# Queueing the filling work of the scan behind the step's pieces on VectorE, ScalarE and GpSimd as well as on TensorE

## The chip, the core and the metric

The program runs on one core of one Trainium2 chip, in one launch. The metric is device microseconds of one execution. Five engines work side by side, each through its own queue of instructions in a fixed order: TensorE (PE in the profile; PEld is its weight load), VectorE (DVE), ScalarE (ACT), GpSimd (POOL), and SyncE (SP), which here only issues DMAs. An instruction starts when those ahead of it on its engine have started and what it waits for on other engines is done.

## The reference

Two layers of a hybrid encoder over 512 tokens of width 1024. Each layer runs three mixers on one projection of the normalised input, multiplies their concatenated output with `w_out`, and then runs a mixture of 16 experts and a small gate. The part that matters here:

```
y_a = gmlp_spatial_gating(...)            # channels 0..255 of the mixers' output
y_b = dilated_attention(...)              # channels 256..639, 6 heads
y_c = gated_deltanet(...)                 # channels 640..1023, 6 heads, forward and backward scan
x = x + concat([y_a, y_b, y_c]) @ w_out[i]
x = x + expert_choice_ffn(rmsnorm(x, g_ffn[i]), ...)
x = x + rmsnorm(p[i] @ w_ple) * sigmoid(rmsnorm(x) @ w_ple_gate)

def step(state, inp):                     # the scan: each step needs the state of the one before
    v_new = u_n - w_n @ state
    o_n = (q_n * exp(g_n)) @ state + qk_n @ v_new
    state = state * exp(g_last) + (k_n * exp(g_last - g_n)).T @ v_new
```

## The kernel before

Each layer's mixer ends in a scan of 16 steps (chunks of 32 tokens, both directions at once). A step is a chain over four engines, and has too little work to fill any of them, so other work is traced between its pieces. `gdn_scan` is the lead. A step n is three pieces: (1) TensorE multiplies the state with keys and queries (`pK`), VectorE scales it (`tm`) and subtracts it from the values (`rr`); (2) TensorE makes `pV`, ScalarE copies it to `vn`; (3) GpSimd scales the state (`St`, line 961), TensorE makes `pS` and `pO`, VectorE adds into `St` and makes `tmp` or `o_sum`, and from step 8 on GpSimd adds `tmp` into `o_sum` (line 988).

The fill is a chain of three generators: `attn_v` (the attention's values), `core` (the attention: scores `sc`, softmax `P`, transposes `ptp`/`PT`, output `po`, split `yTb`), and `w_out_first`, which multiplies the part of the output that the scan does not make (channels 0..639) with `w_out`. `w_out_first` takes its weights in three pieces of 384, 384 and 256 columns (below: pieces 1, 2 and 3; 128x1920, 128x1920 and 128x1280 elements in SBUF). Pieces 4 and 5 (128x1536 each) are for the scan's own channels, in `w_out_last`. At the start of each piece `wnext` splits the raw weights `w` into a high part `whi` (ScalarE, line 338) and the rest `wlo` = w - whi (GpSimd, line 340), and asks for the next raw piece by DMA. A product with a split operand is three matmuls, by `whi` (line 348), by `wlo` (349), and by `whi` again (350), into the PSUM tile `op`; VectorE adds `op` to `x` (line 1039).

`interleave` pulls three pieces of the fill, and then, after each piece of the lead, as much fill as it owes by a table of weights. What it pulls is traced at once. A scheduler then orders each engine's queue by its own model of time; it may move an instruction ahead of others that were traced before it. `in_order` puts a bound on that for TensorE alone: each piece is traced under `issue_after(last)`, where `last` is the TensorE instruction that the piece before ended with, so on TensorE the pieces stand in the order in which they were pulled. On VectorE, ScalarE and GpSimd nothing holds the order, other than data and buffers.

After the scan, `gdn_out` squares `o_sum` (ScalarE, `sqo`, line 1005), sums it (VectorE, `so`, line 1006), takes a reciprocal root by small VectorE steps (lines 183 to 190, result `ro`), scales and gates `o_sum` (1014, 1015), and transposes it (`ycp`, `yTc`). `w_out_last` then multiplies with pieces 4 and 5, and router and experts follow. All weights share a pool of 12 SBUF slots, which are reused as they come free; ScalarE's split of piece 4 and of piece 5 writes into such a slot.

Of the kernel before, what the change touches and what calls it, by code (L numbers as in the profile page):

```python
# [117 lines left out]
class K:  # L118
# [315 lines left out]

    def in_order(self):

        last = None

        def piece(gen):
            nonlocal last  # L440
            with ExitStack() as st:
                if last is not None:
                    st.enter_context(self.tc.issue_after(last))
                r = next(gen, None)
            ins = self.nc.cur_bb.bb.instructions
            k = len(ins) - 1
            while ins[k] is not last and ins[k].engine != self.nc.tensor.engine:
                k -= 1
            last = ins[k]
            return r  # L450

        return piece

    def interleave(self, lead, fill):


        piece, owed = self.in_order(), 0.0
        for _ in range(INIT):
            piece(fill)
        while True:  # L460
            r = piece(lead)
            if r is None:
                return
            owed += r
            while owed > OWED:
                r = piece(fill)
                if r is None:
                    break
                owed -= r
# [1034 lines left out]
```

## Time and profile before

| what | value |
|---|---|
| three timed runs, median (lowest to highest) | 1958.14 us (1953.76 to 1958.29) |
| the profiled execution, device time | 1962.08 us |
| its span, first to last instruction | 1960.3 us |
| PE busy | 1809.5 us, 92% |
| DVE busy | 931.7 us, 48% |
| ACT busy | 523.9 us, 27% |
| POOL busy | 457.4 us, 23% |
| the chain that ended last, by engine | PE 69%, DVE 20%, ACT 3%, POOL 2% |

The scan with its fill stands at about 228 to 382 us of the span in the first layer and 1196 to 1346 us in the second; the experts take most of the rest. In the rows below, times are microseconds from the start of the span. In a timeline each row is one instruction or a few equal ones in sequence: start, duration from the first's start to the last's end, engine, line, operation, tiles and shapes; in square brackets stands how long the engine was idle before it and what ended that. A window's row gives each engine's busy time in the stretch, and PEclk is the granted TensorE clock as a share of 2.4 GHz: 1.00 is 2.4 GHz, 0.50 is 1.2 GHz, and a value between is a mean over both.

### The profile page before, as it was taken

The page shows a single profiled execution, that of the slowest core. Times are in us where ns is not written, and L with a number is a line of the kernel's source. Part 1 is how long each engine was busy: PE and PEld are TensorE (multiplying, and loading weights), DVE is VectorE, ACT ScalarE, POOL GpSimd, SP SyncE. Part 2 cuts the span into 40 slices and gives each one's busy share as a digit, 9 for nine tenths or more (in the row PEclk, how much of TensorE's full clock was granted, in tenths as well). Part 3 has the DMA queues.
Part 4 walks back from the last instruction along what each step waited for, and adds up shares of the span by engine and source line. Part 5 has one row for each costly group of instructions (what it writes and reads, how often), then busy time and mean ns, then how long its engine had stood idle before and what let it go on. Part 6 is the DMA issues. An engine that isn't in the chain of part 4 may idle for free.

```text
span 1960.3 us, 30038 instructions
## 1 busy us (share of the span) xinstructions
PE 1809.5 (92%) x12216; PEld 1140.4 (58%) x12216; DVE 931.7 (48%) x2088; ACT 523.9 (27%) x1213; POOL 457.4 (23%) x402
## 2 busy tenths in 40 slices
PE   6898698979999999999989978899799999999999
PEld 5777665864344444434988767568544344443358
DVE  5879767671112121132778796776511212114126
ACT  4334444331010101102443344552311011011023
POOL 3544313320000003021645452233100000031025
PEclk9998788989999999999998977999799999999999
DMA  5212020187799999899342020202987999998991
GB/s 169 86 33 60 17 85 15 56 329 302 321 423 421 409 421 407 345 412 379 111 134 76 24 74 2 97 2 102 411 321 318 422 421 397 422 394 345 380 328 66
DMA packets 122394, 467.47 MB, mean 238 GB/s; under 512 B 11664, under 2 KB 68496, under 8 KB 75920
## 3 DMA queue, kind: packets, MB, share of 16 engines
q1 hardware_dynamic: 115168, 458.46, 59.5%
q10 hardware_dynamic: 7088, 7.09, 1.2%
q8 instruction: 96, 1.57, 0.3%
q14 instruction: 42, 0.34, 0.1%
HBM read 461.32 MB, written 4.19 MB: 237 GB/s over the span
## 4 chain that ended last, share of the span: by engine, by line
PE 69%; DVE 20%; ACT 3%; issue 3%; POOL 2%; DMA 2%; ACTq 0%; SPq 0%; DVEq 0%; POOLq 0%
PE pGt L1276 14%; PE pUp L1276 11%; PE pY L1276 10%; DVE acc L778 3%; PE xep L1206 2%; PE ysc L1295 2%; DVE rr L944 2%; PE xep L1207 2%; PE pY L1391 2%; PE pV L951 1%; PE op L348 1%; PE ysc L1296 1%; PE pgp L348 1%; PE pgp L350 1%; PE plep L1172 1%
## 5 line engine op out<-in xcount | busy, mean ns | idle before, releaser
L1276 PE MATMUL pGt<-w,xe 128*64 128x512 f32 x592 | 194.8, 607 | 0.0
L340 POOL TENSOR_TENSOR wlo<-w,whi 128x512 fp32r<-128x512 f32 (+5 forms) x66 | 162.1, 2473 | 102.9 <-ACT whi L338 71.9
L1276 PE MATMUL pUp<-w,xe 128*64 128x512 f32 x688 | 178.4, 593 | 0.0
L1343 POOL TENSOR_TENSOR x<-x,hh 128x1024 f32<-128x1024 f32 x8 | 18.8, 2356 | 620.0 <-DMA wx<-in_w_e_up_dram 310.4
L1276 PE MATMUL pY<-w,hidT 128*64 128x512 f32 x608 | 162.5, 596 | 0.2 <-ACT hidT L1350 0.2
L1360 DVE SCALAR_TENSOR_TENSOR yl<-pY,gsl,yh 128x512 fp32r<-128x512 f32 x28 | 21.0, 751 | 203.1 <-ACT yh L1359 201.5
L1301 DVE TENSOR_TENSOR x<-ysc,x 128x512 f32<-128x512 f32 x96 | 62.9, 686 | 110.5 <-PE ysc L1296 110.5
L1276 PEld LDWEIGHTS pUp<-w,xe 128*64 128x64 f32 x688 | 62.9, 137 | 89.5 <-issue 86.3
L1276 PEld LDWEIGHTS pGt<-w,xe 128*64 128x64 f32 x592 | 56.1, 137 | 99.2 <-issue 92.7
L1276 PE MATMUL pGt<-wx,xe 128*64 128x512 f32 x384 | 113.0, 599 | 0.3
L1334 DVE SCALAR_TENSOR_TENSOR hid<-sg,gsl,pUp 128x512 f32<-128x512 f32 x32 | 23.9, 748 | 169.8 <-PE pUp L1276 168.0
L1276 PEld LDWEIGHTS pY<-w,hidT 128*64 128x64 f32 x608 | 55.6, 136 | 76.2 <-issue 73.3
L1276 PE MATMUL pUp<-wx,xe 128*64 128x512 f32 x320 | 99.8, 595 | 0.0
L1276 PE MATMUL pY<-wx,hidT 128*64 128x512 f32 x288 | 86.2, 595 | 0.0
L1327 DVE SCALAR_TENSOR_TENSOR sg<-sg,pGt 128x512 f32<-128x512 f32 x32 | 21.7, 686 | 131.3 <-ACT sg L1326 131.3
L338 ACT ACTIVATE whi<-w 128x512 fp32r<-128x512 f32 (+5 forms) x66 | 68.2, 1058 | 38.5 <-PE op L349 15.8
L1326 ACT ACTIVATE sg<-pGt,gsl 128x512 f32<-128x512 f32 x32 | 21.8, 687 | 196.5 <-PE pGt L1276 194.6
L1350 ACT ACTIVATE hidT<-htp 128x512 f32<-128x512 f32 x32 | 19.0, 597 | 200.4 <-PE htp L1349 200.4
L1206 PE MATMUL xep<-OH,hh 128*128 128x256 f32 x256 | 70.1, 307 | 2.4 <-DVE OH L1194 2.4
L778 DVE SCALAR_TENSOR_TENSOR acc<-raw,pp,acc 128x512 f32<-128x512 f32 x72 | 64.3, 894 | 15.5 <-ACT acc L776 13.0
L348 PE MATMUL pgp<-whi,gTh 128*128 128x256 f32 x256 | 70.9, 281 | 0.0
L350 PE MATMUL pgp<-whi,gTl 128*128 128x256 f32 x256 | 69.8, 282 | 0.3 <-DVE gTl L279 0.3
(404 smaller groups left out, 4277.3 us busy)
## 6 DMA issues: line engine op xcount, KB each, us to landing
w<-in_w_e_up_dram SPq DMA_DIRECT2D x86, 1024.0 KB, 15.4
w<-in_w_e_down_dram SPq DMA_DIRECT2D x76, 1024.0 KB, 12.7
w<-in_w_e_gate_dram SPq DMA_DIRECT2D x74, 1024.0 KB, 15.6
wx<-in_w_e_gate_dram SPq DMA_DIRECT2D x48, 1024.0 KB, 9.9
wx<-in_w_e_up_dram SPq DMA_DIRECT2D x40, 1024.0 KB, 16.7
wx<-in_w_e_down_dram SPq DMA_DIRECT2D x36, 1024.0 KB, 12.0
wd<-in_w_e_down_dram SPq DMA_DIRECT2D x32, 512.0 KB, 8.3
w<-in_w_in_dram SPq DMA_DIRECT2D x14, 1024.0 KB, 5.2
```

The lines of the kernel that those rows point to most:

```text
L338: self.nc.scalar.activation(rr_(hi[:, ks, :]), wk, AF.Copy)
L340: e.tensor_tensor(rr_(lo[:, ks, :]), wk, hi[:, ks, :], op=ALU.subtract)
L348: pe.matmul(p, lh, rh, start=first, stop=False)
L350: pe.matmul(p, ll, rh, start=False, stop=last)
L778: v.scalar_tensor_tensor(acc, raw[:, kk:kk + S], conv[:, b, kk:kk + 1], acc, op0=ALU.mult, op1=ALU.add)
L944: v.tensor_tensor(rr[kl[dr], :], vtok[kl[dr], tl, :], fl(tm[kl[dr]]), op=ALU.subtract)
L1206: pe.matmul(p, rr_(hh[:, t, ks]), OHf[:, t, :], start=(t == 0), stop=False)
L1207: pe.matmul(p, rr_(hl[:, t, ks]), OHf[:, t, :], start=False, stop=(t == NT - 1))
L1276: pe.matmul(pt[nh][64 * ei:64 * ei + 64, :], lhs[:, kk, 64 * ei:64 * ei + 64], wt[ei][k][:, nh * 512:nh * 512 + 512], start=(kk == 0), sto ...
L1295: pe.matmul(p, rr_(OT[:, t, :]), rr_(yh[:, ns]), start=True, stop=False)
L1301: v.tensor_tensor(xv, p, xv, op=ALU.add)
L1391: pe.matmul(pY[64 * ei:64 * ei + 64, :], hidT[:, 4 * half + k, 64 * ei:64 * ei + 64], wt[ei][:, k, :], start=(half + k == 0), stop=(half * ...
```

## The change

`in_order`'s `piece` gets a flag that says whether the piece is the lead's. After a piece of the lead it notes the last instruction that the piece traced on VectorE, on ScalarE and on GpSimd. Each later piece of the fill is traced under `issue_after` for these three too, so its instructions on an engine queue behind the last piece of the lead that was pulled before it. The lead's own pieces get no such bound against the fill. On TensorE the rule is as before.

```diff
-        last = None
-
-        def piece(gen):
+        last, ahead = None, {}
+
+        def piece(gen, leads=False):
             nonlocal last
+            ins = self.nc.cur_bb.bb.instructions
+            k0 = len(ins)
             with ExitStack() as st:
                 if last is not None:
                     st.enter_context(self.tc.issue_after(last))
+                if not leads:
+                    for i in ahead.values():
+                        st.enter_context(self.tc.issue_after(i))
                 r = next(gen, None)
...
+            for i in ins[k0:]:
+                if i.engine == self.nc.tensor.engine:
+                    last = i
+                elif leads and i.engine in (self.nc.vector.engine, self.nc.scalar.engine, self.nc.gpsimd.engine):
+                    ahead[i.engine] = i
             return r
...
-            r = piece(lead)
+            r = piece(lead, True)
```

Behind `in_order` all line numbers are 8 higher in the changed kernel. What the bound does to the queues is best seen where `w_out_first` starts. On GpSimd, before, the first rows of the scan hold the splits of pieces 1 and 2 (`wlo` 128x1920), among the state's scalings of steps 1 to 9:

```order
L961 TENSOR_TENSOR St<-St,ex 128x384 x5
L340 TENSOR_TENSOR wlo<-w,whi 128x1920
L961 TENSOR_TENSOR St<-St,ex 128x384 x2
L340 TENSOR_TENSOR wlo<-w,whi 128x1920
L961 TENSOR_TENSOR St<-St,ex 128x384 x2
L988 TENSOR_TENSOR o_sum<-tmp,o_sum 32x384 x2
```

and the scan's last rows there, with the splits of pieces 3, 4 and 5, are

```order
L961 TENSOR_TENSOR St<-St,ex 128x384
L988 TENSOR_TENSOR o_sum<-tmp,o_sum 32x384 x2
L340 TENSOR_TENSOR wlo<-w,whi 128x1280
L961 TENSOR_TENSOR St<-St,ex 128x384
L988 TENSOR_TENSOR o_sum<-tmp,o_sum 32x384 x4
L340 TENSOR_TENSOR wlo<-w,whi 128x1536
L988 TENSOR_TENSOR o_sum<-tmp,o_sum 32x384 x2
L340 TENSOR_TENSOR wlo<-w,whi 128x1536
```

In the changed kernel GpSimd's first nine scalings stand in a row, and all five splits are in the scan's last rows:

```order
L969 TENSOR_TENSOR St<-St,ex 128x384
L996 TENSOR_TENSOR o_sum<-tmp,o_sum 32x384 x2
L340 TENSOR_TENSOR wlo<-w,whi 128x1920
L969 TENSOR_TENSOR St<-St,ex 128x384
L996 TENSOR_TENSOR o_sum<-tmp,o_sum 32x384 x4
L340 TENSOR_TENSOR wlo<-w,whi 128x1920
L340 TENSOR_TENSOR wlo<-w,whi 128x1280
L340 TENSOR_TENSOR wlo<-w,whi 128x1536
L996 TENSOR_TENSOR o_sum<-tmp,o_sum 32x384 x2
L340 TENSOR_TENSOR wlo<-w,whi 128x1536
```

Piece 1 moved past eight scalings to the place behind step 12's `o_sum`, piece 2 to the place behind step 14's, and pieces 3 and 4 now stand ahead of the `o_sum` of step 15, the last one. On ScalarE the copies of step 12 (the `vn` at the head) are followed, before, by the attention's last exponential and its copies:

```order
L955 ACTIVATE vn<-pV 32x384 x2
L632 ACTIVATE P,smx<-P,mx 128x512
L642 ACTIVATE PT<-ptp 128x512 x2
L277 ACTIVATE yTb<-po 128x128
L642 ACTIVATE PT<-ptp 128x512
```

and in the changed kernel by the high part of piece 1 first:

```order
L963 ACTIVATE vn<-pV 32x384 x2
L338 ACTIVATE whi<-w 128x1920
L640 ACTIVATE P,smx<-P,mx 128x512
L650 ACTIVATE PT<-ptp 128x512 x2
L277 ACTIVATE yTb<-po 128x128
```

The weight split moved from far ahead to the row ahead of the exponential. At the end of the scan ScalarE's queue holds, before, steps 13 to 15 with the high part of piece 4 among them, the four squares of `gdn_out`, and the high part of piece 5:

```order
L955 ACTIVATE vn<-pV 32x384 x4
L338 ACTIVATE whi<-w 128x1536
L955 ACTIVATE vn<-pV 32x384 x2
L1005 ACTIVATE sqo<-o_sum 128x384 x4
L338 ACTIVATE whi<-w 128x1536
L277 ACTIVATE yTc<-ycp 128x3x128 x2
```

and in the changed kernel

```order
L963 ACTIVATE vn<-pV 32x384 x6
L338 ACTIVATE whi<-w 128x1920
L338 ACTIVATE whi<-w 128x1280
L338 ACTIVATE whi<-w 128x1536
L1013 ACTIVATE sqo<-o_sum 128x384 x3
L338 ACTIVATE whi<-w 128x1536
L1013 ACTIVATE sqo<-o_sum 128x384
L277 ACTIVATE yTc<-ycp 128x3x128 x2
```

The high part of piece 2 moved behind the last step's `vn`, and the last square moved behind the high part of piece 5. The second layer's rows are the same. On TensorE the order of the scan and its fill is as before, apart from the order of 12 `pS` matmuls in a few steps; the 15 `op` matmuls that stand between `pV` and `pO` of the last step are the first that use piece 2, in both kernels. On VectorE a few rows of steps 4 to 6 and 12 changed places, and the last step's order with `gdn_out`; steps 8 to 11 are as before. SP's queue is the same. In the experts and at the end of the layers a few neighbouring rows changed places.

## Rows read from the trace of the kernel before

**Rows 1.** Chain of waits, `pV` of steps 4, 8 and 12 in both layers (start, us, what)
```profile
267.26 0.85 PE pV L951 x22
...
316.75 0.85 PE pV L951 x24
...
351.70 0.87 PE pV L951 x22
...
1235.93 0.85 PE pV L951 x22
...
1281.01 0.79 PE pV L951 x24
...
1315.90 0.87 PE pV L951 x22
```

**Rows 2.** Windows by stage (busy PE, PEld, DVE, ACT, POOL, PEclk, DMA share, GB/s)
```profile
262.00:318.00 56.00, 47.59 (x608) 31.71 (x605) 41.07 (x108) 24.25 (x53) 13.19 (x7) 0.79 0.14 49
318.00:352.00 34.00, 31.79 (x510) 21.36 (x510) 27.79 (x83) 18.89 (x44) 11.48 (x12) 1.00 0.01 2
...
402.00:422.00 20.00, 20.00 (x111) 16.91 (x110) 12.03 (x43) 6.95 (x14) 0.80 (x2) 1.00 1.00 399
...
1230.00:1282.00 52.00, 43.59 (x630) 29.59 (x629) 41.61 (x110) 24.73 (x53) 13.19 (x7) 0.87 0.17 61
```

**Rows 3.** Timeline of DVE, the subtraction `rr` of three steps
```profile
275.14 3.86 DVE L944 TENSOR_TENSOR rr<-vtok,tm 32x384 f32<-32x384 f32 x2
...
290.33 1.13 DVE L944 TENSOR_TENSOR rr<-vtok,tm 32x384 f32<-32x384 f32 x2
...
299.07 5.05 DVE L944 TENSOR_TENSOR rr<-vtok,tm 32x384 f32<-32x384 f32 x2
```

**Rows 4.** Timeline of POOL, splits of pieces 1, 2, 3, 5 and one `o_sum`
```profile
273.77 4.24 POOL L340 TENSOR_TENSOR wlo<-w,whi 128x1920 fp32r<-128x1920 f32 x1 [0.35 <-ACT whi L338]
...
299.12 4.59 POOL L340 TENSOR_TENSOR wlo<-w,whi 128x1920 fp32r<-128x1920 f32 x1 [2.73 <-issue]
...
356.33 2.06 POOL L988 TENSOR_TENSOR o_sum<-tmp,o_sum 32x384 f32<-32x384 f32 x2
359.65 3.07 POOL L340 TENSOR_TENSOR wlo<-w,whi 128x1280 fp32r<-128x1280 f32 x1 [1.26 <-PE po L649]
...
391.45 3.52 POOL L340 TENSOR_TENSOR wlo<-w,whi 128x1536 fp32r<-128x1536 f32 x1 [6.61 <-ACT whi L338]
```

**Rows 5.** Timeline of PE, second layer: the wait of step 7's `pV`
```profile
1269.79 1.48 PE L951 MATMUL pV<-rr,XT 32*32 32x64 f32 x22 [3.95 <-DVE rr L944]
```

**Rows 6.** Timeline of ACT: a split, `vn` of steps 12 and 15, piece 5
```profile
271.89 1.81 ACT L338 ACTIVATE whi<-w 128x1920 fp32r<-128x1920 f32 x1
...
352.59 0.99 ACT L955 ACTIVATE vn<-pV 32x384 f32<-32x384 f32 x2 [1.14 <-PE pV L951]
...
378.43 0.99 ACT L955 ACTIVATE vn<-pV 32x384 f32<-32x384 f32 x2 [0.26 <-PE pV L951]
...
389.83 1.49 ACT L338 ACTIVATE whi<-w 128x1536 fp32r<-128x1536 f32 x1 [2.82 <-PE op L349]
```

**Rows 7.** Timeline of PE: first `wlo` matmuls of pieces 1 and 2, last `pO`
```profile
359.63 0.34 PE L349 MATMUL op<-wlo,yTa 128*128 128x384 f32 x1
...
378.54 0.33 PE L349 MATMUL op<-wlo,yTa 128*128 128x384 f32 x1
...
381.08 0.86 PE L977 MATMUL pO<-vn,QKm 32*32 32x64 f32 x24
```

**Rows 8.** Timeline of DVE in `gdn_out`: last `so`, a held and the last step of `ro`
```profile
387.88 0.54 DVE L1006 TENSOR_REDUCE so<-sqo 128x6 f32<-128x384 f32 x1
...
392.13 2.88 DVE L190 SCALAR_TENSOR_TENSOR ro__4169<-nr,ro__4169 128x24 f32<-128x24 f32 x1
...
395.71 0.18 DVE L1011 SCALAR_TENSOR_TENSOR ro__4169<-ro__4169,rk 128x24 f32<-128x24 f32 x1
```

**Rows 9.** Timeline of PE: `w_out_last`'s first matmul
```profile
400.07 0.50 PE L348 MATMUL op<-whi,yTc 128*128 128x512 f32 x1 [0.23 <-DVE o_sum L1015]
```

More of the change, by code (lines that the diff above doesn't have):

```diff
@@ L443, in piece @@
                     st.enter_context(self.tc.issue_after(last))
+                if not leads:
+                    for i in ahead.values():
+                        st.enter_context(self.tc.issue_after(i))
                 r = next(gen, None)
[L445 to L449, printed above, removed]
+            if ins is not self.nc.cur_bb.bb.instructions:
+                raise RuntimeError("block")
+            for i in ins[k0:]:
[3 more added lines that the diff above has]
+                    ahead[i.engine] = i
             return r
```

## The prediction

> **What bounds the kernel now.** I read the windows by stage first, then the chain of waits through the scan, then the timelines of VectorE and GpSimd where the chain lingers, and last the timelines around the start of `w_out_first` and of `gdn_out`.
>
> In the scan TensorE is nearly always busy, but not always at full clock. From `pV` of step 8 to `pV` of step 12 the first layer takes 351.70 - 316.75 = 34.95 us and the second 1315.90 - 1281.01 = 34.89 us, or 8.73 us a step, at 2.4 GHz [rows 1, 2]. The four steps before that, with the same fill, take 49.49 and 45.08 us [rows 1]. So something costs 14.5 us in the first layer and 10.2 us in the second, and only there.
>
> It shows on VectorE: the two subtractions `rr` of a step take 1.13 us as a rule, but 3.86 and 5.05 us in two steps [rows 3]. Those two start while GpSimd subtracts the big `wlo`, 273.77 to 278.01 and 299.12 to 303.71, and end 0.4 to 1.0 us behind it [rows 3, 4]; the second layer has the same pair. `pV` needs `rr`, and TensorE, whose order is fixed, stands idle for up to 3.95 us [rows 5]. After such waits the granted clock is at its lower level for a while: its mean over these stretches is 0.79 and 0.87, against 1.00 in the four steps behind [rows 2]. As a share of time at 1.2 GHz that is 2 x 0.21 x 56 = 23.5 us and 2 x 0.13 x 52 = 13.5 us, some 9 us for each of the four waits. Held `rr` and lower clock together are the 14.5 and 10.2 us.
>
> **The change part by part.** By the queues, VectorE's order is nearly unmoved; what moves is the splits of pieces 1 to 4.
>
> Gain: pieces 1 and 2 leave the middle of the scan, so both held `rr` and what follows go. I take all of it: 14.5 + 10.2 = 24.7 us. The bounds are the held time alone, (3.86 - 1.13) + (5.05 - 1.13) = 6.65 us a layer [rows 3], 13.3 in all, and 27 if the short splits on ScalarE counted too. What is late next there is TensorE's own fill, at 8.73 us a step.
>
> First new wait, step 13. Step 12's `vn` ends at 353.58; the split of piece 1 takes 1.81 us behind it [rows 6], and queued behind that on ScalarE are the last exponential, two `PT` and a `yTb`, on which the last `ptp` and `po` wait, so TensorE comes 1.8 us later to `op`. GpSimd's `o_sum` ends at 358.39, and only then `wlo` starts and takes 4.24 to 4.59 us [rows 4], to 362.6 or 363.0. The first matmul by `wlo` stood at 359.63 [rows 7]. It comes 3.2 us late, with everything behind it on TensorE. Bounds: 1.8 (ScalarE's part alone), and 3.2 + 4.6 if the clock falls too (9 us at half clock). I take 3.2: the longest single pause is some 2 us, nearer to the short pauses (2.2 us in all) that the stretch from 318 to 352 has at clock 1.00 than to 3.95 [rows 2, 5].
>
> Second new wait, step 15. Step 15's `vn` ends at 379.42. Then come 1.81 us of `whi` and 4.24 to 4.59 of `wlo` for piece 2 [rows 4, 6]; with two hand-overs of 0.07 us, as from a split's end at 273.70 to the `wlo` at 273.77, that is 385.4 to 385.9, say 385.7. The first matmul that needs it stood at 378.54 [rows 7], so TensorE stands for 7.2 us, but for one matmul. Queued behind it are 14 more `op` and the scan's last `pO`, and behind `pO` the whole of `gdn_out`. The wait is longer than any after which the clock fell, so I take 1.2 GHz for 9 us from 385.7. The 14 `op` took (381.08 - 378.54) = 2.54 us [rows 7] and now take 5.1, which puts `pO` at 390.8. From `pO` to the end of piece 2's matmuls, which the split of piece 5 waits for, it was 389.83 - 381.08 = 8.75 us [rows 6, 7]; with 3.9 us of it still at half pace it is 10.7, and the split starts at 401.5 and ends at 403.0. The last square, which stood ahead of it, is now behind it on ScalarE: `so` ends near 404.1, where it was 388.42 [rows 8]. `wlo` of piece 5 then holds GpSimd from 403.1 to 406.6 [rows 4], and a small VectorE step was held for 2.88 us by this very subtraction [rows 4, 8]. Before, that hit the middle of the root, and `ro` was done at 395.89; now it hits its first step, with some 18 small steps behind it, 0.2 us each with their gaps [rows 8], so `ro` is done at 406.6 + 3.6 = 410.2, 14.3 us late. Two adds into `x` that stood between `ro` and `w_out_last` are done earlier; I count them at 0.4 us each, a little less than `so`. So `w_out_last` starts at 400.07 + 14.3 - 0.8 = 413.6 [rows 9]: 13.5 us late. With the clock up, the same sum gives `pO` at 388.2, the split at 397.0, `ro` at 405.7 and 9.0 us late. These are the ends; pieces 3 and 4, subtracted at 385.7 to 392.3 (3.07 + 3.52 us [rows 4]), hide behind the late `pO`, and would cost 1 us more with the clock up. The next weights' DMA, behind piece 5's on SP, comes some 10 us late too; it goes along with the late experts.
>
> One rule is weighed here. No row shows a reduction on VectorE beside a GpSimd subtraction; if `so` were held as `rr` is, its 0.54 us [rows 8] would come behind `wlo` instead of beside it, 1.1 us more over both layers, and I leave that out. The Trainium skill, "SBUF — State Buffer", section "Who interferes with whom", says that a two-input VectorE instruction contends with GpSimd's reads and that a tensor_reduce on trn2 never does; by that the sum stays as it is, and no row here shows the reduction's half of it.
>
> Then `w_out_last`. TensorE has finished `w_out_first` at about 409 and waits 4 us for `gdn_out`, as long as the waits after which the clock fell. TensorE is busy without a gap in the 20 us that follow [rows 2], so 9 us at half clock would cost up to 4.6 us, and none if it stays up. About half of the lower-clock loss came through in the scan: (14.5 - 6.65) of 11.8, (10.2 - 6.65) of 6.8. I take 2.5 a layer.
>
> Small things: fewer splits ahead of exponentials, `vn` ahead of `att` in the first steps, some swaps on VectorE and among the experts. None has a row; the bounds are 3 us a layer gained (both 1.8 us splits in full) and 2 lost. I take 1 gained, less than one split.
>
> Sum: 2 x (3.2 + 13.5 + 2.5 - 1) - 24.7 = 36.4 - 24.7 = 11.7 us slower. The profiled execution took 1962.08 us (span 1960.3), so 1973.8 there; it lay 3.9 us above the median of the runs, 1958.14, and against that the change gives **1970 us**.
>
> **The rivals.**
> - Not slower: the clock stays at 2.4 GHz through the waits at steps 13 and 15 and before `w_out_last`. The price is then 2 x (3.2 + 9.0 - 1) = 22.4 us against 24.7: 1956, and 1953 if step 13 costs only 1.8. It decides if TensorE's `op` matmuls behind the wait run in 0.18 us each from the start. For it: pauses that add up to 2.2 us in 34 left the clock at 1.00 [rows 2]. Against: 7.2 us of standing is twice what came before each fall. Chance 0.20.
> - More slowly: the clock falls at step 13 too, and the fall in `w_out_last` costs all of 4.6 us. That adds 2 x (4.6 + 2.1) = 13.4: 1983. For it: around the wait TensorE is idle in three pauses close together. Chance 0.18.
> - The gain fails: without held `rr` the four steps are still long, since TensorE's fill bounds them. Then 13.3 of 24.7 us come: 1981. Against: steps 8 to 12 run the same fill in 8.73 us [rows 1]. Chance 0.10.
> - What the change says, the step's own pieces first on VectorE and ScalarE, shortens every step. With 0.5 us (about one `rr`) in each of 11 steps a layer that is 11 us back: 1959. Against: VectorE's queue is unmoved in steps 8 to 11. Chance 0.10.
>
> **How the numbers follow.** The forecast has 0.42, with its own range of 1962 to 1978. A measurement of this kernel can tell about 0.3% from no change, 5.9 us: faster is under 1952.3, slower over 1964.0. Slower: 0.39 of the forecast's 0.42, the second and third rival, and 0.02 of the fourth: 0.69. Faster: 0.08 of the first and 0.03 of the fourth: 0.11. The same: 0.20. The range for 8 in 10 goes from 1954, the better part of the first rival, to 1984, the second.
>
> **What would show it.** Right: no `rr` over 1.5 us in steps 4 to 8 and clock 1.00 there, 35 us from `pV` of step 4 to step 8 in both layers; a pause of 4 us ahead of `op` by `wlo` in step 15, below clock 1.00 behind it; the last `sqo` behind `whi` of piece 5; `w_out_last` 17 us later after step 12's `pV` than the 48.4 us before. Wrong: `op` matmuls of piece 2 that don't wait, a clock of 1.00 from step 13 to the router, or long steps 4 to 8 without a held `rr`.

## The result and the profile after

The changed kernel takes 1969.74 us (median of four runs, 1967.44 to 1975.43), where the kernel before takes 1957.43 (four runs beside it, 1953.76 to 1958.29). The ratio, of the means, is 1.0071, with a 95% interval of 1.0046 to 1.0096: 12.3 us slower. The forecast was 1970, 11.7 us slower.

The profiled execution of the changed kernel took 1975.43 us (span 1973.6), 13.3 us more of span than before. Of these, 4.4 lie ahead of the first matmul by `gs` (`pexp`, at 92.69 before and 97.13 after), where no instruction has moved; in all profiled runs below it stands at 92.3 to 93.8. So that much is this one execution's own, and most of the 5.7 us by which it stands above its median.

The chain of waits of the changed kernel (start, us, what), `pV` of steps 4, 8 and 12 in both layers, as in [rows 1]:

```profile
272.38 0.85 PE pV L959 x22
...
307.20 0.85 PE pV L959 x22
...
341.68 0.87 PE pV L959 x22
...
1241.94 0.85 PE pV L959 x22
...
1275.44 0.85 PE pV L959 x22
...
1310.39 0.87 PE pV L959 x22
```

Steps 4 to 8 now take 34.82 and 33.50 us instead of 49.49 and 45.08. Windows of the same stretches and of the scan's end (columns as in [rows 2]):

```profile
272.00:280.00 8.00, 7.77 (x117) 5.13 (x118) 4.93 (x16) 3.25 (x8) 0.78 (x1) 0.79 0.01 2
280.00:308.00 28.00, 26.65 (x442) 17.85 (x433) 23.86 (x75) 14.51 (x34) 2.65 (x4) 1.00 0.01 2
...
374.00:384.00 10.00, 6.31 (x40) 5.41 (x40) 0.56 (x1) 2.60 (x2) 9.84 (x3) 0.55 0.01 3
...
1242.00:1276.00 34.00, 32.52 (x540) 21.94 (x541) 28.42 (x90) 17.86 (x43) 3.42 (x4) 1.00 0.01 3
```

Where the clock was 0.87, in the second layer, it is 1.00. In the first layer, where it was 0.79, it is 0.79 for the first 8 us still, and 1.00 from 280 on. GpSimd (the last engine in the row) is busy for 3 us instead of 13. The price stands at 374 to 384: GpSimd works through three splits without a break, and TensorE is busy for 6.3 us of 10 at a granted clock of 0.55. TensorE there:

```profile
374.01 0.69 PE L348 MATMUL op<-whi,yTa 128*128 128x384 f32 x1 [2.82 <-ACT whi L338]
378.38 0.69 PE L349 MATMUL op<-wlo,yTa 128*128 128x384 f32 x1 [3.68 <-POOL wlo L340]
...
383.12 0.86 PE L985 MATMUL pO<-vn,QKm 32*32 32x64 f32 x24
```

ScalarE and GpSimd at the same place:

```profile
371.29 0.97 ACT L963 ACTIVATE vn<-pV 32x384 f32<-32x384 f32 x2 [6.82 <-PE pV L959]
372.17 2.94 ACT L338 ACTIVATE whi<-w 128x1920 fp32r<-128x1920 f32 x2
...
391.85 1.49 ACT L338 ACTIVATE whi<-w 128x1536 fp32r<-128x1536 f32 x1 [0.85 <-PE op L349]
393.24 0.51 ACT L1013 ACTIVATE sqo<-o_sum 128x384 f32<-128x384 f32 x1
```
```profile
374.08 10.64 POOL L340 TENSOR_TENSOR wlo<-w,whi 128x1920 fp32r<-128x1920 f32 x3 [5.09 <-issue]
...
393.47 3.52 POOL L340 TENSOR_TENSOR wlo<-w,whi 128x1536 fp32r<-128x1536 f32 x1 [6.57 <-ACT whi L338]
```

(On ScalarE the row x2 is `whi` of pieces 2 and 3, on GpSimd the row x3 is `wlo` of pieces 2, 3 and 4.) The last `vn` ends at 372.26; `whi` of piece 2 follows it, then `wlo`, and TensorE gets to the first `op` by `wlo` at 378.38, 6.1 us behind `vn`. VectorE in `gdn_out`:

```profile
394.15 0.54 DVE L1014 TENSOR_REDUCE so<-sqo 128x6 f32<-128x384 f32 x1
394.73 2.30 DVE L1015 TENSOR_TENSOR so<-so,rk 128x24 f32<-128x24 f32 x1
```

Both lie beside the `wlo` of piece 5 (393.47 to 396.99): the reduction takes its usual 0.54 us, and the next small step ends only with `wlo`. One thing came that the prediction had not seen. The DMA of the router's weights (`wr`), issued by ScalarE behind `yTc`, and the experts' first weights (`wx`), issued by SyncE; first before, then after:

```profile
399.88 0.39 ACTq L1071 DMA_DIRECT2D wr<-in_w_router_dram  x1
...
400.56 2.01 SPq L1264 DMA_DIRECT2D wx<-in_w_e_gate_dram  x4
...
402.24 0.41 POOL L1074 TENSOR_TENSOR wr<-wr,pp 128x128 f32<-128x128 f32 x1 [6.93 <-DMA wr<-in_w_router_dram]
```
```profile
404.77 2.15 SPq L1272 DMA_DIRECT2D wx<-in_w_e_gate_dram  x4
...
404.96 0.39 ACTq L1079 DMA_DIRECT2D wr<-in_w_router_dram  x1
...
419.09 0.40 POOL L1082 TENSOR_TENSOR wr<-wr,pp 128x128 f32<-128x128 f32 x1 [21.76 <-DMA wr<-in_w_router_dram]
419.54 1.06 PE L1110 MATMUL pl<-wr,xT 128*128 128x16 f32 x8 [1.56 <-POOL wr L1082]
...
1390.05 1.89 PE L1110 MATMUL pl<-wr,xT 128*128 128x16 f32 x8 [2.50 <-POOL wr L1082]
```

Issued 0.7 us ahead of 4 MB of expert weights, `wr` landed in 2.3 us; issued 0.2 us behind their first, it took 14.1, and the router's first `pl` waits 1.56 us for it in the first layer and 2.50 in the second.

Stage by stage, from the profiled executions (us; sums over both layers, forecast from the prediction's terms):

| stage | layer 1 | layer 2 | measured | forecast |
|---|---|---|---|---|
| `pV` of step 4 to step 8 | 49.49 to 34.82 | 45.08 to 33.50 | -26.2 | -24.7 |
| `pV` of step 12 to `w_out_last` | 48.37 to 63.23 | 48.65 to 64.18 | +30.4 | +33.4 |
| `w_out_last` to the router's last `pl` | 30.3 to 32.3 | 28.9 to 36.6 | +9.6 | +5.0 |
| everything else | | | -0.5 | -2.0 |
| sum | | | +13.3 | +11.7 |

"Everything else" is +4.4 at the start of the span, +4.1 from `pV` of step 3 to step 4 (+3.3 and +0.9), -3.8 in the first step of the first layer's scan, -5.3 from the first `pGt` to the layer's end (-0.9 and -4.4), and small sums of either sign. For the -3.8 (granted clock 1.00 instead of 0.61) nothing was tested. In the profiled executions the six kernels that bound the fill as a whole, or on GpSimd alone, take 8.9 to 9.2 us for this step, and of the six others five take 12.6 to 12.8 and one, the kernel before in fifths, 9.1.

### The profile page after: what moved, and what is told of

Same layout as the page of the kernel before. It is cut to its first block, busy times and chain, and to the rows that moved or that the text cites. A ratio compares the mean times of both kernels' runs of the same rounds, so it can differ in the third digit from the quotient of the medians.

```text
span 1973.6 us, 30032 instructions
## 1 busy us (share of the span) xinstructions
PE 1801.5 (91%) x12216; PEld 1140.2 (58%) x12216; DVE 917.9 (47%) x2088; ACT 524.1 (27%) x1213; POOL 457.6 (23%) x402
## 4 chain that ended last, share of the span: by engine, by line
PE 66%; DVE 20%; ACT 4%; issue 4%; DMA 4%; POOL 3%; SPq 0%; ACTq 0%; DVEq 0%; POOLq 0%
PE pGt L1284 14%; PE pUp L1284 11%; PE pY L1284 10%; DVE acc L786 3%; PE xep L1214 2%; PE ysc L1303 2%; PE xep L1215 2%; DMA wr<-in_w_router_dram 1%; PE plep L1180 1%; PE pgp L350 1%; PE ysc L1304 1%; PE pY L1399 1%; PE pgp L348 1%; PE pgp L349 1%; PE pV L959 1%
## 5 line engine op out<-in xcount | busy, mean ns | idle before, releaser
L1284 PEld LDWEIGHTS pUp<-w,xe 128*64 128x64 f32 x688 | 62.2, 137 | 88.9 <-issue 86.2
L349 PE MATMUL pgp<-wlo,gTh 128*128 128x256 f32 x256 | 71.9, 285 | 0.0
## 6 DMA issues: line engine op xcount, KB each, us to landing
w<-in_w_e_down_dram SPq DMA_DIRECT2D x76, 1024.0 KB, 13.3
```

The lines of the kernel that those rows point to most:

```text
L349: pe.matmul(p, lh, rl, start=False, stop=False)
L1284: pe.matmul(pt[nh][64 * ei:64 * ei + 64, :], lhs[:, kk, 64 * ei:64 * ei + 64], wt[ei][k][:, nh * 512:nh * 512 + 512], start=(kk == 0), sto ...
```

## The experiments

Times are medians; a ratio is to the kernel before on the same chip, with its 95% interval. Stages are counted here from the first `pV` matmul of a step, in the profiled executions: from step 4 to step 8 the kernel before takes 49.9 and 45.5 us in the two layers, the changed one 34.8 and 33.5; from step 12 to `w_out_last` 48.9 and 49.2, and 63.6 and 64.7. With the bound kept for VectorE alone (a program that was not timed) every engine's queue is that of the kernel before, row for row: the change acts through ScalarE and GpSimd.

**The bound for the splits alone.**
```diff
+        self.ahead = ahead
...
-                if not leads:
-                    for i in ahead.values():
-                        st.enter_context(self.tc.issue_after(i))
...
         for c0, cols in WO_COLS:
-            wh, wl = self.wnext()
+            with ExitStack() as st:
+                for i in self.ahead.values():
+                    st.enter_context(self.tc.issue_after(i))
+                wh, wl = self.wnext()
```


> Of the change only one thing is done: the weight splits of pieces 1 to 3 (whi on ScalarE, wlo on GpSimd) queue behind the scan's pieces pulled before them; all other filling work is free as in the kernel before. Theory (the moved splits are the whole change): 34 to 36 us from pV of step 4 to pV of step 8 in both layers, the first matmul by wlo of piece 2 some 6 us behind the last vn, clock below 1.00 there, and 1964 to 1974 us; a little under the changed kernel if it counts that o_sum of step 15 stands ahead of the splits of pieces 3 and 4 here. Rival (the order of the attention's exponentials and copies makes the difference): 1955 to 1960 us.

1973.58 us, ratio 1.0068 (1.0046 to 1.0089), as the change. Steps 4 to 8 take 33.5 us in both layers, step 12's `pV` to `w_out_last` 65 us, and the first `op` by `wlo` of piece 2 has the same pause of 3.67 us. So the moved splits are the change, but for one price: from `pV` of step 3 to step 4 it is 8.8 us here in both layers, as before, where the changed kernel has 12.0 and 9.7. The last `o_sum` stood ahead of the splits of pieces 3 and 4 here and it made nothing quicker.

**The kernel before, its splits in fifths.**
```diff
-            wh, wl = self.wnext()
+            wh, wl = self.wnext(pieces=5)
```


> The kernel before, with the splits of pieces 1 to 3 cut into five parts each (wlo 128x384 instead of 128x1920); their place in the queues stays. Theory (a GpSimd subtraction holds VectorE's rr until that one instruction ends): the longest rr of steps 4 to 8 is 1.13 + 0.85 = 2 us instead of 3.86 and 5.05, pV of step 4 to step 8 takes 35 to 38 us, the clock stays near 1.00, and the time is 1957 - 2 x (8 to 11) = 1935 to 1941 us. Rival 1 (VectorE gets no turn between subtractions that follow each other): rr as long as before, 1955 to 1959 us. Rival 2 (the lower clock there does not come from the held rr): only the 13.3 us of held time come back, 1943 to 1946 us.

1935.67 us, ratio 0.9874 (0.9849 to 0.9899): faster than both kernels. VectorE and GpSimd around steps 5 and 7, against [rows 3, 4]:

```profile
272.68 1.88 DVE L944 TENSOR_TENSOR rr<-vtok,tm 32x384 f32<-32x384 f32 x2
285.13 1.13 DVE L944 TENSOR_TENSOR rr<-vtok,tm 32x384 f32<-32x384 f32 x2
294.70 1.82 DVE L944 TENSOR_TENSOR rr<-vtok,tm 32x384 f32<-32x384 f32 x2
```
```profile
270.92 5.45 POOL L340 TENSOR_TENSOR wlo<-w,whi 128x384 fp32r<-128x384 f32 x5
...
294.75 5.69 POOL L340 TENSOR_TENSOR wlo<-w,whi 128x384 fp32r<-128x384 f32 x5 [2.73 <-issue]
```

The five parts follow each other for 5.5 us, and `rr` still gets its turn: 1.9 and 1.8 us instead of 3.9 and 5.1. That is the theory's number (2), and rival 1 has fallen. Steps 4 to 8 take 39.8 and 35.3 us. The difference is the clock; windows of 16 us from step 5 on in either layer:

```profile
270.00:286.00 16.00, 14.29 (x156) 9.05 (x155) 11.46 (x30) 7.96 (x19) 7.07 (x7) 0.68 0.00 1
1224.70:1240.70 16.00, 14.29 (x227) 9.40 (x225) 14.12 (x40) 11.20 (x26) 7.07 (x7) 1.00 0.01 2
```

Both layers have the same two pauses of TensorE there, 0.80 and 0.91 us; in the first the clock fell behind them, in the second it did not. The run with pieces 4 and 5 in thirds (the last one below) has the same two pauses in both layers, stays at 1.00 in both and takes 35.3 us each. So these pauses alone do not decide whether the clock falls; what does is open. Rival 2 has fallen with the time: 23 us came back, not 13.3.

**Finer still.** `wlo` in tenths (128x192):
```diff
-                e.tensor_tensor(rr_(lo[:, ks, :]), wk, hi[:, ks, :], op=ALU.subtract)
+                for c in range(halves):
+                    cs = slice(c * cols // halves, (c + 1) * cols // halves)
+                    e.tensor_tensor(rr_(lo[:, ks, cs]), wk[:, :, cs], hi[:, ks, cs], op=ALU.subtract)
...
-            wh, wl = self.wnext()
+            wh, wl = self.wnext(pieces=5, halves=2)
```


> The kernel before with the splits of pieces 1 to 3 in still smaller parts: whi in fifths, wlo in tenths (128x192). Theory (rr waits for no more than the one GpSimd subtraction that runs): the longest rr of steps 4 to 8 is 1.13 + 2 x 0.5 us at most and nearer to 1.6, where fifths gave 1.88; TensorE's two pauses of 0.8 and 0.9 us at step 5 shrink by half and the clock no longer falls in the first layer, which gives back the 4.5 us by which its steps 4 to 8 (39.8 us) were longer than the second layer's (35.3); 1929 to 1934 us. Rival (each part has a fixed cost on GpSimd, and smaller parts hold rr as often as fifths): 1934 to 1939 us.

1936.81 us, ratio 0.9901 (0.9869 to 0.9933), no better than fifths. The mechanism is as expected (longest `rr` 1.76 us, steps 4 to 8 34.8 us in both layers, no fall of the clock in the profiled execution), but the time is the rival's. The profiled execution gains 5.5 us on that of fifths in these steps and loses as much elsewhere: 3.5 us in the first step of the first layer's scan (12.6 us against 9.1) and 3.0 between the layers. What makes these two was not tested, so why the median is no better is open.

**The same subtraction on VectorE.**
```diff
-            wh, wl = self.wnext()
+            wh, wl = self.wnext(pieces=5, dve=1)
```


> The kernel before, with the wlo of pieces 1 to 3 made by VectorE in five parts of 128x384, which the scheduler places among the scan's VectorE work; GpSimd has no subtraction until piece 4. Theory (GpSimd's subtraction beside rr is the cost, and VectorE has room in the scan, 24 to 28 us of 35 busy): five parts of 0.56 us are 2.8 us a piece on VectorE, no rr waits for longer than that, pV of step 4 to step 8 takes 35 to 38 us, and the time is 1933 to 1942 us. Rival (VectorE is the bound of those steps, and 2.8 us more on it come through): 1950 to 1960 us.

1949.15 us (1938.63 to 1952.70), ratio 0.9941 (0.9921 to 0.9962). Steps 4 to 8 take 41.7 and 42.8 us, between theory and rival. No `rr` is held (1.13 us each), but the five parts stand ahead of step 5's `rr` in VectorE's queue, and `pV` waits 3.69 us for it; the granted clock from step 4 to step 8 is 0.88. The collision is gone, its place is taken by the order.

**The router's weights ahead of the experts', in the changed kernel.**
```diff
-        nc.scalar.dma_start(wr, A["w_router"]...
+        nc.sync.dma_start(wr, A["w_router"]...
```


> The changed kernel, with the DMA of the router's weights issued by SyncE ahead of the experts' first weights instead of by ScalarE, 0.2 us behind them. Theory (the 14 us from issue to landing are the queueing behind 4 MB of expert weights, and TensorE's waits of 1.56 and 2.50 us ahead of the first pl, with the lower clock behind the second one, come from that): landing within 3 us, no wait ahead of pl, from w_out_last's first matmul to the router's last pl 30 us in both layers instead of 32.3 and 36.6, and the time 3 to 8 us under the changed kernel's 1969.7. Rival (the wait is covered by the experts' weights or by the chain of rmsnorm): within 2 us of 1969.7. Rival (the DMA holds SyncE's queue and so the experts' weights): up to 3 us slower.

1964.50 us, ratio 1.0020 (1.0004 to 1.0035), against 1.0071 with ScalarE's issue. `wr` lands 4.7 us after its issue, no `pl` waits, and `w_out_last` to the last `pl` takes 30.3 and 28.7 us, as before the change. So 5 us by the medians, 0.5% by the ratios, of the change's loss are this DMA's place behind the burst: with `gdn_out` late, the order of the two queues had turned.

**The changed kernel, its splits in fifths.**
```diff
-            wh, wl = self.wnext()
+            wh, wl = self.wnext(pieces=5)
```


> The changed kernel, with the splits of pieces 1 to 3 cut into five parts each (whi and wlo 128x384 instead of 128x1920), in the same places of the queues. Theory (the wait of step 15 is the length of one whole split, whi and then wlo): the first matmul by wlo of piece 2 comes about 1.5 us behind the last vn instead of 6.1, the following ones at the pace of the parts (about 1.1 us each on GpSimd), the last pO 3 to 5 us earlier, from pV of step 12 to w_out_last 59 to 62 us instead of 63.6 and 64.7, and the time 1960 to 1965 us. Rival (the matmuls wait for the whole tile): the wait is as long or 1 to 2 us longer, 1970 to 1974 us.

1961.99 us, ratio 1.0023 (1.0010 to 1.0037). TensorE behind the last `vn` (which ends at 368.87):

```profile
369.33 0.69 PE L348 MATMUL op<-whi,yTa 128*128 128x384 f32 x1 [1.54 <-ACT whi L338]
370.47 0.69 PE L349 MATMUL op<-wlo,yTa 128*128 128x384 f32 x1 [0.45 <-POOL wlo L340]
```

The wait went from 6.1 us to 1.6, and step 12's `pV` to `w_out_last` takes 58.5 and 60.7 us (59 to 62 expected). Matmuls wait for their part only, and the wait of step 15 is the length of a whole split.

**Pieces 2 and 3 split half a piece earlier, in the changed kernel.**
```diff
+        nxt = self.wnext()
         for c0, cols in WO_COLS:
-            wh, wl = self.wnext()
+            wh, wl = nxt
...
+                if t == 1 and c0 != WO_COLS[-1][0]:
+                    nxt = self.wnext()
```


> The changed kernel, with the splits of pieces 2 and 3 pulled half a piece earlier, behind the second of the four token tiles of the piece before; the bounds of the change stay. Theory (the wait of step 15 comes from the place where the split is pulled, and with it the late root and w_out_last): no wait ahead of op by wlo of piece 2, 34 us from pV of step 4 to step 8 as in the changed kernel, 52 to 57 us from pV of step 12 to w_out_last (49 before, 3 for the wait of step 13, up to 5 for an rr of step 14 or 15 that is held by the subtraction), and the time 1946 to 1956 us. Rival (the held rr of step 15 and the lower clock behind it cost as much as the wait): 1962 to 1972 us.

1963.55 us, ratio 1.0029 (1.0010 to 1.0049): a miss, and the rival's case. No `op` waits any more, but the two subtractions now run where step 14 subtracts; VectorE and then GpSimd:

```profile
357.66 7.80 DVE L952 TENSOR_TENSOR rr<-vtok,tm 32x384 f32<-32x384 f32 x2
```
```profile
357.63 7.42 POOL L340 TENSOR_TENSOR wlo<-w,whi 128x1920 fp32r<-128x1920 f32 x2
```

One `rr` waited for the `wlo` of piece 2, the next for that of piece 3, TensorE stood for 2.70 and 2.79 us, and step 12's `pV` to `w_out_last` takes 62.2 us in both layers. What it gains on the change lies in the main behind the scan: 28.3 and 28.8 us from `w_out_last` to the last `pl`, against 32.3 and 36.6.

**GpSimd's bound alone.**
```diff
-                elif leads and i.engine in (self.nc.vector.engine, self.nc.scalar.engine, self.nc.gpsimd.engine):
+                elif leads and i.engine == self.nc.gpsimd.engine:
```


> Of the change only the bound on GpSimd is kept; on ScalarE and VectorE the filling work is free as before, so that whi of pieces 1 to 3 comes early and only wlo is late. Theory (the gain needs only GpSimd's bound, the wait of step 15 needs ScalarE's): 34 us from pV of step 4 to step 8; wlo of piece 2 starts behind the o_sum of step 14 without waiting for whi, some 5 us earlier than in the changed kernel; TensorE waits 0 to 2 us there, 52 to 58 us from pV of step 12 to w_out_last, and the time 1945 to 1957 us. Rival (GpSimd's place alone makes the wait): 62 to 65 us from pV of step 12 to w_out_last, 1965 to 1972 us.

1968.35 us, ratio 1.0057 (1.0035 to 1.0078): a miss too. The gain came in full (33.5 us from step 4 to step 8 in both layers), so GpSimd's bound is enough for it. But step 12's `pV` to `w_out_last` takes 68.0 and 63.7 us. In the first layer step 13's `rr` is held for 4.90 us by the `wlo` of piece 1. `wlo` of piece 2 did start 5 us sooner after its `o_sum`, at 367.94, and so a moment ahead of the last `rr` (368.01), which it and the `wlo` of piece 3 held for 7.73 us. Neither theory nor rival had these collisions. In the changed kernel ScalarE's late `whi` keeps `wlo` off that `rr`, and so the wait for `whi` costs little on balance (1.4 us by the medians).

**All repairs of the changed kernel together** (early, in fifths, router's weights first; the edits are those above).

> The changed kernel with three edits: splits of pieces 1 to 3 in five parts, those of pieces 2 and 3 pulled half a piece earlier, and the router's weights issued by SyncE ahead of the experts' first weights. Theory (the change's gain of 26 us stays, and each of its prices goes): 34 us from pV of step 4 to step 8, 50 to 54 us from pV of step 12 to w_out_last, 29 to 31 us from there to the router's last pl, and 1932 to 1942 us, about the time of the kernel before with its splits in five parts. Rival (the splits hold rr of steps 13 to 15 and the scan's last steps pay): 1945 to 1955 us.

1949.88 us, ratio 0.9965 (0.9950 to 0.9979): better than before, but the rival's time. `rr` of steps 14 and 15 takes 2.68 and 2.53 us beside the parts, and step 12's `pV` to `w_out_last` 58.4 and 58.7 us, not 50 to 54. In the first layer the granted clock over this stretch is 0.91, where fifths in their old place have 1.00 over 48.8 us: the lower clock is worth up to 0.09 x 58.4 = 5.3 us, about half of the difference.

**Pieces 4 and 5 in thirds, on top of the fifths in the kernel before.**
```diff
-            self.wo2 = [self.wnext() for _ in range(2)]
+            self.wo2 = [self.wnext(pieces=3) for _ in range(2)]
```


> The kernel before with the splits of pieces 1 to 3 in fifths, and those of pieces 4 and 5 in thirds (128x512). Theory (the step of the root that was held for 2.88 us by the whole wlo of piece 5 waits for one part of 1.2 us only): w_out_last starts 1 to 2 us earlier in each layer (47 to 48 us behind pV of step 12 instead of 48.8), 1932 to 1935 us where fifths alone gave 1935.7. Rival (between parts only one small VectorE step gets its turn, so the chain of 18 waits for all three parts): 48.8 us or more, 1935 to 1939 us.

1937.64 us, ratio 0.9902 (0.9872 to 0.9931), and 48.9 us to `w_out_last`: no gain, the rival's case. The root's chain beside the three parts:

```profile
375.24 0.17 DVE L188 TENSOR_TENSOR nr<-ro__4201 128x24 f32<-128x24 f32 x1
375.45 1.24 DVE L189 TENSOR_TENSOR nr<-nr 128x24 f32<-128x24 f32 x1
376.73 1.21 DVE L190 SCALAR_TENSOR_TENSOR ro__4201<-nr,ro__4201 128x24 f32<-128x24 f32 x1
377.98 1.20 DVE L188 TENSOR_TENSOR nr<-ro__4201 128x24 f32<-128x24 f32 x1
379.21 0.20 DVE L189 TENSOR_TENSOR nr<-nr 128x24 f32<-128x24 f32 x1
```

Between two parts exactly one small step gets its turn, so a chain of short steps waits for every part, where a single `rr` waits for one or two.

## Why the prediction was right

**The gain** was forecast as 14.5 + 10.2 = 24.7 us and came as 14.7 + 11.6 = 26.2. Its reason is shown, not only argued: in the changed kernel no `rr` of steps 4 to 8 takes over 1.13 us, and cutting the splits in their old place brings nearly the same stretch (39.8 and 35.3 us, or 34.8 twice with tenths). The third rival (only 13.3 us come) has fallen with both. Not all was clean: step 4's `pV` comes 12.0 us behind step 3's in the first layer and 9.7 in the second (8.8 before). In the first there is a new pause of 2.15 us for its `rr`, where VectorE's order of steps 4 to 6 had moved, and behind it the clock of 0.79 from 272 to 280; with it steps 4 to 8 take 34.82 us, without it, in the second layer, 33.50. I took VectorE's order for nearly unmoved and did not price these 4.1 us, so the gain net of them is 22.1. One reading of [rows 3, 4] was loose too: of each pair only one `rr` is held. In step 7 the first starts 0.05 us ahead of `wlo` and takes its usual 0.56 us, and the second waits.

**The wait of step 13** was forecast as 3.2 us, by GpSimd's late `wlo`. From step 12's `pV` (341.68) to the first `op` by `wlo` (352.49) it takes 10.8 us, where it was 359.63 - 351.70 = 7.9: 2.9 us late, and 3.7 in the second layer. The size was nearly right, but by luck, since the path was another one. TensorE and GpSimd there, and the clock in both layers:

```profile
346.76 1.09 PE L657 MATMUL po<-PT,att 128*64 128x128 f32 x16 [1.75 <-ACT PT L650]
...
352.49 0.34 PE L349 MATMUL op<-wlo,yTa 128*128 128x384 f32 x1
```
```profile
347.97 4.24 POOL L340 TENSOR_TENSOR wlo<-w,whi 128x1920 fp32r<-128x1920 f32 x1
```
```profile
346.00:352.00 6.00, 4.50 (x60) 3.63 (x60) 2.86 (x7) 2.04 (x5) 5.84 (x3) 0.74 0.01 3
1314.00:1322.00 8.00, 5.78 (x61) 4.76 (x61) 3.66 (x9) 2.76 (x7) 6.76 (x4) 0.57 0.02 3
```

No `op` waits for `wlo`, which is done at 352.21 (in the second layer 1.4 us before the first `op` by it). TensorE is late by the 1.75 us that it waits for `PT`, behind ScalarE's split, which the prediction had as its lower bound of 1.8, and by a lower clock behind that wait, in both layers, which it had put at nothing.

**The wait of step 15** was forecast as 13.5 us to the start of `w_out_last`, 16.7 with step 13's; the two together came as 14.9 and 15.5. The order was as forecast all the way: `wlo` 6.1 us behind `vn` (6.3 forecast), 14 `op` at half pace, the last `sqo` behind `whi` of piece 5, the root's first step held by the `wlo` of piece 5. The term is 1.2 to 1.8 us too large, mainly because the lower clock was taken for 9 us from the first `op` by `wlo` on. It began while TensorE still stood (granted 1.00 from 371 to 372, 0.50 from 373 on) and ended at `pO` (383.12), so only 4.7 us of it fell on these matmuls: from `pO` to the split of piece 5 it takes 391.85 - 383.12 = 8.7 us, the 8.75 of full clock, where I had put 10.7.

**`w_out_last`'s lower clock** was forecast as 2.5 us a layer. The stage cost 2.0 and 7.7, and for another reason in the main. The clock did fall at its start (0.83 and 0.86 over the first 6 us), but that fall cost next to nothing by the stage's end. Windows from `w_out_last` to the last `pl` in both layers, in the kernel before, in the changed one, and in the one with the router's weights ahead (columns as in [rows 2]):

```profile
400.07:430.41 30.34, 30.25 (x175) 26.40 (x175) 17.73 (x68) 11.29 (x25) 0.80 (x2) 0.93 0.98 385
1364.55:1393.49 28.94, 28.85 (x175) 25.04 (x175) 17.73 (x68) 11.30 (x25) 0.80 (x2) 0.98 0.98 382
```
```profile
404.91:437.21 32.30, 30.74 (x176) 26.38 (x175) 17.12 (x66) 11.46 (x25) 0.80 (x2) 0.92 0.93 352
1374.57:1411.18 36.61, 34.11 (x176) 29.55 (x175) 17.12 (x66) 11.46 (x25) 0.80 (x2) 0.83 0.92 354
```
```profile
400.94:431.21 30.27, 30.27 (x176) 26.27 (x175) 17.14 (x66) 11.46 (x25) 0.40 (x1) 0.92 0.98 390
1370.32:1398.98 28.66, 28.66 (x176) 25.08 (x175) 17.14 (x66) 11.46 (x25) 0.40 (x1) 0.97 0.97 389
```

With the router's weights ahead the stage begins at 0.58 and 0.87 over 6 us, and its mean clock and its length are still those of the kernel before, which has a lower stretch of its own later in the first layer (0.51 from 426 to 431). What the changed kernel loses is the late `wr`: 1.56 and 2.50 us of waiting, and in the second layer a lower clock behind it (0.52 from 1391 to 1397; 0.83 over the stage). Here the working failed: the prediction weighed the next weights' DMA on SyncE's queue only, and not that the late `gdn_out` would turn the order of two queues. Without that DMA's delay the stage costs nothing against before, and the change is slower by 0.2%, not 0.7%. So the term of 2.5 a layer came to nothing, and a wait that the prediction had left out stood in its place. (Its factor was loose as well: 7.85 of 11.8 us and 3.55 of 6.8 are 0.67 and 0.52, not "about half" of both.)

**Small things** were put at -2 us and came at about -5 in this one execution, leaving the 4.4 us at its start aside; of that, the 4.1 us ahead of step 4's `pV` are a price, the 3.8 gained in the scan's first step may be the change's or the clock's chance, and the experts' rows that changed places were not tested, so what makes the rest is open.

So the sum was right partly by luck: one term came by another path than the one it gave, one came to nothing, and the misses made up for each other. The gain was 1.5 us better, the waits 3.0 cheaper and the small things 2.9 better, against 4.6 more behind `w_out_last` and the 4.4 us at the start of this one execution. Of the rivals, the first (the clock stays up) is refuted by 0.55 at 374 to 384 us; the second (the clock falls at step 13 too) happened in both layers (0.74 and 0.57 above), but its price did not: `op` came 2.9 and 3.7 us late, where that rival has 3.2 + 4.6; the fourth (every step shorter) is not seen, since steps 8 to 12 take 34.5 and 35.0 us as before.

The rule of the Trainium skill that was weighed ("SBUF — State Buffer", "Who interferes with whom") holds in this trace on both sides: `so` by reduction takes 0.54 us beside `wlo`, and the next step, with two inputs in SBUF, 2.30.

## What to carry to other kernels

A bound that puts the critical chain first on an engine only helps if the work that it holds back is not needed soon after: look up, for each delayed instruction, who waits for it and what is left to cover that. Where a long instruction on one engine holds a short one on another, cut the long one before moving it: five parts in the old place brought 1.3% with no new wait, while every other place that was tried for the whole split met another `rr` or made TensorE wait. And a stage that becomes late also turns the order between DMA queues; a small transfer behind a burst of large ones is worth pinning ahead of it.

## What the runs showed of the hardware

- A VectorE instruction with two inputs in SBUF that starts beside a GpSimd subtraction waits until that one instruction ends, whatever its own size: 128x24 steps take 2.30 to 2.88 us, and where the subtraction is cut into three, three steps in a row take 1.2 us each. Between two parts exactly one of them gets its turn. An `rr` that started 0.05 us ahead of `wlo` took its usual 0.56 us, and that `wlo` 4.59 instead of 4.24.
- Not all wait. `so` by reduction (0.54 us) and the additions `x` = `op` + `x`, with one input in PSUM (0.42 us), run at their usual length beside the same `wlo`. A 128x24 step with one tensor input and constants does wait (GpSimd's `wlo` from 384.55 to 388.06 in the run with all repairs):

```profile
384.89 0.42 DVE L1048 TENSOR_TENSOR x<-op,x 128x256 f32<-128x256 f32 x1 [0.41 <-PE op L350]
385.24 2.86 DVE L186 TENSOR_SCALAR ro__4193<-nr 128x24 int32<-128x24 int32 x1
```

- The same 64 KB DMA took 2.3 us from issue to landing when issued 0.7 us ahead of 4 MB on another queue, and 14.1 us when issued 0.2 us behind its start. A small lead is not enough: ahead by 0.36, 0.30 and 0.10 us in other runs (splits half a piece earlier; bound for the splits alone, second layer; changed kernel in fifths, second layer), it took 5.8, 8.3 and 13.4 us.
